# Mixture of experts behind a ring of weights: the overflow test moves into the up product

## The chip, the cores and the metric

One NeuronCore of a Trainium2 chip runs the whole program. The metric is the device time of one execution in microseconds. Before the change three runs took 1918.42, 1920.21 and 1922.09 us; the median is 1920.21.

## The reference, cut to what matters

The program is three transformer layers over 256 tokens of width 1024 in float32: a windowed attention layer and a short convolution layer, each with a feed-forward part, and a third layer with two kinds of attention and a mixture of 32 experts. The change touches the experts alone. Each token goes to 4 of 32 experts; tokens of one expert are gathered, multiplied with its up weights (1024 x 2048), put through a gated activation, multiplied with its down weights (1024 x 1024), weighted and added back:

```python
logits = (xf @ w_router + b_router)
top_v, top_i = lax.top_k(logits, TOP_K)          # 4 of 32
w = jax.nn.softmax(top_v, axis=-1)
...
h = lax.ragged_dot(xs, w_up, sizes) + b_up[sorted_e]
g, lin = jnp.split(h, 2, axis=-1)
g = jnp.minimum(g, SWIGLU_LIMIT)
lin = jnp.clip(lin, -SWIGLU_LIMIT, SWIGLU_LIMIT)
act = g * jax.nn.sigmoid(SWIGLU_ALPHA * g) * (lin + 1.0)
y = lax.ragged_dot(act, w_down, sizes) + b_down[sorted_e]
y = y * w.reshape(-1)[order][:, None].astype(y.dtype)
return jax.ops.segment_sum(y, tok, num_segments=n).reshape(B, T, D)
```

## The kernel before

All large weights pass through one ring of slots in SBUF (class Ring, lines 24 to 76). A unit is 128 partitions x 4096 floats, 2048 KB. An expert has six units: four of up weights (moe_u[e, 0] to moe_u[e, 3]; except in expert 0, unit c holds k steps 2c and 2c+1 of all columns) and two of down weights (moe_u[e, 4] and [e, 5]). While the experts run, the ring has ten slots. The units have a fixed order. Line 53 issues their transfers from SyncE; a unit is issued when the program has given a slot back (ring.done) and the last reader of the slot's old tile is done. What SyncE has to wait for is a semaphore that the reader raises; a reader inside a conditional block counts as done when the block has been left.

The loop over the experts (lines 1947 to 1978) is written out 32 times. For expert e it computes, on up to 64 tokens:

- the up product (up, line 1724): bias, then 8 k steps into the PSUM banks pg (gate) and pl (linear), each step with two column halves in two halves of the rows; 64 products of 512 columns;
- combine(pem): adds the output of expert e-1 to the accumulators (eight products);
- extra(e, 0), lines 1814 to 1856: a conditional block on the token count in a register. If the expert has more than 64 tokens, rounds of 32 further tokens are computed from the same units, with all six of them. TensorE, VectorE and ScalarE each take this branch for themselves;
- ring.done for the four up units (line 1964), then act_g and act_l on VectorE and ScalarE (lines 1738 to 1745);
- slot_dup (line 1750) writes a one-hot table ohb, and gather_part gathers half of the tokens of a later pair of experts on TensorE, with the step on line 1712 behind it on VectorE;
- act_T transposes the activation (line 1778), the copy on line 1971 writes atm; slot_T (line 1761) transposes the one-hot table and copies it to pem (line 1762); slot_w (line 1769) multiplies the slots' weights and reduces them to wslm;
- the down product (down) with its bias, then weigh (lines 1799 and 1800).

The overflow code writes pem, wslm, yh and yl, the same tiles as the main path. Of the 32 experts one has an overflow round, the ninth (number 8; counted from 0).

Two limits stand in the issues of SyncE: eight transfers at most are under way, since each issue waits for one of eight semaphores in turn, and ten slots at most are held.

Of the kernel before, what the change touches and what calls it, by code (L numbers as in the profile page):

```python
# [8 lines left out]
F32R = mybir.dt.float32r  # L9
# [3 lines left out]
ALU = mybir.AluOpType  # L13
AX = mybir.AxisListType
ET = mybir.EngineType
P = 128
# [117 lines left out]
def kernel(ctx: ExitStack, tc: tile.TileContext, a: dict, out: bass.AP):  # L134
# [100 lines left out]
    ring = Ring(nc, ringp, RING)  # L235
# [145 lines left out]
    moe_u = {}  # L381
# [43 lines left out]
    def mm(o, l, r, start, stop):  # L425
        T.matmul(o, l, r, start=start, stop=stop)  # L426
# [1256 lines left out]
    def m2(name, shape, dt=F32, bufs=1):  # L1683
        return p2.tile(list(shape), dt, tag=name, bufs=bufs, name=name)
# [24 lines left out]
    def gather_part(gi, part, bank="ps"):  # L1709
        ps = X[bank].rearrange("p (a b) -> p a b", a=4)  # L1710
        gather(ps, ohs[gi], 4 * part, 4, 128)
        V.tensor_tensor(xgs[gi % 2][:, 4 * part:4 * part + 4], ps, gain2(4 * part, 4, 128), op=ALU.mult)

    def wk(e, c, k, h):

        if (e, c) == (31, 4):
            return v8(512)(ring.take(moe_u[e, c + h]))[:, k]
        if c == 4 or e == 0:
            u = ring.take(moe_u[e, c + k // 4])
            return u.rearrange("p (k f) -> p k f", k=4)[:, k % 4, h * 512:(h + 1) * 512]  # L1720
        u = ring.take(moe_u[e, k // 2])
        return u.rearrange("p (i f) -> p i f", i=2)[:, k % 2, (c // 2 * 2 + h) * 512:(c // 2 * 2 + h + 1) * 512]

    def up(e, cs, xg, free=False):

        ps = [X["pl" if c else "pg"] for c in cs]
        for p_, c in zip(ps, cs):
            for h in range(2):
                mm(p_[h * 64:(h + 1) * 64], oh3[:, e:e + 1].to_broadcast([96, 64]),
                   bup[0:96, (c + h) * 512:(c + h + 1) * 512], True, False)  # L1730
        for k in range(8):
            for p_, c in zip(ps, cs):
                for h in range(2):
                    mm(p_[h * 64:(h + 1) * 64], xg[:, k], wk(e, c, k, h), False, k == 7)
            if free and k % 4 == 3:
                ring.done(moe_u[e, cs[0] + k // 4])

    def act_g(pg, gm, th):
        V.tensor_scalar(gm, pg, 7.0, None, op0=ALU.min)  # L1739
# [3 lines left out]
    def act_l(dst, pl, gm, li):  # L1743
        V.tensor_scalar(li, pl, 7.0, -7.0, op0=ALU.min, op1=ALU.max)
        V.scalar_tensor_tensor(dst, li, 1.0, gm, op0=ALU.add, op1=ALU.mult)  # L1745

    def four(t):
        return t.rearrange("p (q j) -> p q j", j=4)

    def slot_dup(e, io, n):  # L1750

        for tt in range(2):
            V.tensor_scalar(X["ohb"][:, tt].rearrange("p (r s) -> p r s", s=n),
                            io[:, None, :n].to_broadcast([P, 128 // n, n]), posm[:, tt, e:e + 1], None,
                            op0=ALU.is_equal)

    def slot_T(pe, bank="ps"):

        ps = X[bank].bitcast(BF16)[:, 0:256].rearrange("p (a b) -> p a b", a=2)
        for tt in range(2):  # L1760
            T.transpose(ps[:, tt], X["ohb"][:, tt], identb)
        S.copy(pe, ps)  # L1762

    def slot_w(e, wsl, bank="ps"):

        pw = X[bank][:, 256:259]
        for tt in range(2):
            mm(pw, X["ohb"][:, tt], w3[:, tt, e], tt == 0, tt == 1)
        V.tensor_reduce(wsl, pw, axis=AX.X, op=ALU.add)

    def by_rows(ac):

        return ac.rearrange("p (j q) -> p q j", j=4)

    def act_T(ac, bank):
        ps = X[bank].rearrange("p (a b) -> p a b", a=4)
        for j in range(4):
            T.transpose(ps[:, j], ac[:, j * 128:(j + 1) * 128], ident)  # L1778
        return ps
# [15 lines left out]
            for g in range(2):  # L1795
                mm(py[g * 64:(g + 1) * 64], at[:, k, g * 64:(g + 1) * 64], wk(e, 4, 4 * g + k, h), g == 1 and k == 0, k == 3)

    def weigh(wsl):
        S.activation(yy[0], X["py"], AF.Identity, scale=wsl)  # L1799
        V.scalar_tensor_tensor(yy[1], X["py"], wsl, yy[0].bitcast(F32), op0=ALU.mult, op1=ALU.subtract)  # L1800

    def combine(pe):
        for h in range(2):
            for tt in range(2):
                for i in range(2):
                    mm(accm[tt][h], pe[h * 64:(h + 1) * 64, tt], yy[i][h * 64:(h + 1) * 64], False, False)

    def combine_half(pe, h):

        for tt in range(2):  # L1810
            for i in range(2):
                mm(accm[tt][h], pe[:, tt], yy[i], False, i == 1)

    def extra(e, i):

        if i == 6:
            return
        with tc.If(rv > 64 + 32 * i, label=f"extra{e}" if i == 0 else None) as more:  # L1818
            io, xo = X["io"], X["xg"]
            V.tensor_scalar(io, iota1, float(64 + 32 * i), None, op0=ALU.add)  # L1820
            onehot(X["oh"], 1, e, io)
            ps = X["ps"].rearrange("p (a b) -> p a b", a=8)
            gather(ps, X["oh"], 0, 8, 64)
            V.tensor_tensor(xo, ps[:, :, 0:32], gain2(0, 8, 32), op=ALU.mult)
            slot_dup(e, io, 32)
            pu = X["py"]
            for c in range(4):
                mm(pu[c * 32:(c + 1) * 32], oh3[:, e:e + 1].to_broadcast([96, 32]),
                   bup[0:96, c * 512:(c + 1) * 512], True, False)
            for k in range(8):  # L1830
                for c in range(4):
                    mm(pu[c * 32:(c + 1) * 32], xo[:, k], wk(e, c // 2 * 2, k, c % 2), False, k == 7)
            slot_T(pem)
            slot_w(e, wslm)
            S.copy(by_rows(X["li"]), four(pu))
            pt = act_T(X["li"], "ps")
            gm, th, at = [t[:, 0:256].rearrange("p (a b) -> p a b", a=4) for t in (X["th"], X["li"], atm)]
            act_g(pt[:, :, 0:64], gm, th)
            act_l(at, pt[:, :, 64:128], gm, th)
            py = X["py"]  # L1840
            for n in range(2):
                mm(py[64 * n:64 * n + 32], oh3d[:, e:e + 1].to_broadcast([96, 32]), bdn3[:, n * 512:(n + 1) * 512],
                   True, False)
            for kk in range(4):
                for kp_ in range(2):
                    k = 2 * kk + kp_
                    for n in range(2):
                        o = 32 * (2 * n + kp_)
                        mm(py[o:o + 32], at[:, k % 4, (k // 4) * 32:(k // 4 + 1) * 32], wk(e, 4, k, n), kk == 0 and kp_ == 1, kk == 3)
            weigh(wslm)  # L1850
            combine(pem)
            extra(e, i + 1)
        if i == 0 and e < 31:
            with more.Else():
                foresee(e + 1)

    def embed(part):
# [11 lines left out]
        for h in range(2):  # L1869
# [4 lines left out]


    X = {"ps": pstat([P, 512]), "pg": pb(), "pl": pb(), "py": pb(),
         "oh": m2("ohx", [P, 2, 64]), "xg": m2("xgx", [P, 8, 32]), "gm": m2("gm", [P, 512]), "th": m2("th", [P, 512]),
         "li": m2("li", [P, 512]), "ohb": m2("ohb", [P, 2, 128], BF16), "io": m2("io", [P, 64])}
    atm = m2("atm", [P, 512])
    pem = m2("pem", [P, 2, 128], F32R)  # L1880
    wslm = m2("wslm", [P, 1])
    yy = (m2("yh", [P, 512], F32R), m2("yl", [P, 512], F32R))
    xgs = [m2(f"xg{i}", [P, 8, 128]) for i in range(2)]
    ohs = {0: m2("oh", [P, 2, 128], bufs=2)}
    w3 = m2("w3", [P, 2, 32, 3], BF16)
# [61 lines left out]
    for e in range(32):  # L1947
        gi, o = divmod(e, 2)
        xg = xgs[gi % 2][:, :, o * 64:(o + 1) * 64]
        rv = nc.values_load(cnt[0:1, e:e + 1], engines=engs, min_val=0, max_val=256)  # L1950
        assert moe_u[e, 5] in ring.tiles
        if o == 0 and e < 30:
            ohs[gi + 1] = m2("oh", [P, 2, 128], bufs=2)
            onehot(ohs[gi + 1], 2, e + 2, iota1)
        if e == 0:
            extra(0, 0)
            for c in (0, 2):
                up(0, (c,), xg, True)
        else:
            up(e, (0, 2), xg)  # L1960
            combine(pem)
            extra(e, 0)
            for c in range(4):
                ring.done(moe_u[e, c])
        act_g(X["pg"], X["gm"], X["th"])
        act_l(by_rows(X["li"]), four(X["pl"]), four(X["gm"]), four(atm))
        slot_dup(e, iota1, 64)
        if e < 30:
            gather_part(gi + 1, o)
        pt = act_T(X["li"], "pl")  # L1970
        S.copy(atm.rearrange("p (a b) -> p a b", a=4), pt)
        slot_T(pem, "pg")
        slot_w(e, wslm, "pg")
        if e < 31:
            down(e, atm.rearrange("p (a b) -> p a b", a=4))
            weigh(wslm)
            for c in range(4, 6):
                ring.done(moe_u[e, c])
# [195 lines left out]
```

## Time and profile before

| | |
|---|---|
| median of three runs | 1920.21 us |
| profiled execution | 1920.84 us |
| its span | 1919.1 us |
| its mean granted TensorE clock | 0.975 |
| TensorE busy (PE) | 1747.5 us, 91% |
| VectorE (DVE), ScalarE (ACT), GpSimd (POOL) | 44%, 28%, 10% |
| moved by DMA | 581.70 MB, mean 303 GB/s |

The experts take the second half of the span, from about 910 us. A matmul counts as busy while it is in the pipeline, so a high share of PE does not say that PE is what the others wait for; the chain of waits and the idle times do. Rows that end in brackets tell how long the engine had been idle before, and what ended the wait. [...]

### The profile page before, as it was taken

The numbers are of one execution on the slowest core, as the hardware profiler recorded it, in microseconds if no ns is written. First come the engines' busy times: TensorE is split into PE (matmuls) and PEld (weight loads), VectorE is DVE, ScalarE is ACT, GpSimd is POOL, SyncE is SP. The second block draws the span as 40 slices with busy tenths as digits, with TensorE's granted clock in tenths as the row PEclk, the third lists the DMA queues.
The fourth block names the chain that finished last, engine by engine and source line by source line (L and its number), as shares of the span: only waits on it lengthen the run. The fifth ranks groups of instructions, "written<-read, shape, count | busy, mean of one in ns | idle before, by whom it ended". The sixth has DMA issues, their size and how long they took to land. (4 is left out here: it accounts for less than half of the span.)

```text
span 1919.1 us, 30101 instructions
## 1 busy us (share of the span) xinstructions
PE 1747.5 (91%) x12485; PEld 1162.4 (61%) x12487; DVE 836.6 (44%) x1640; ACT 542.2 (28%) x1058; POOL 196.0 (10%) x279
## 2 busy tenths in 40 slices
PE   5989999999999999998999998899988988898886
PEld 4757999989999998868433333343333433333334
DVE  3866677666588886576222211221211211112125
ACT  3455454544355454363000000000000000000004
POOL 2220000000124331402000000000000000000003
PEclk8999999999999999899999998999999999899989
DMA  9675856488776527517799998999999999999980
GB/s 332 223 220 173 299 176 219 155 229 255 229 247 199 181 80 226 151 44 297 318 392 427 424 427 352 388 426 425 426 427 427 426 426 428 424 426 426 427 322 25
DMA packets 160415, 581.70 MB, mean 303 GB/s; under 512 B 8952, under 2 KB 84928, under 8 KB 136400
## 3 DMA queue, kind: packets, MB, share of 16 engines
q1 hardware_dynamic: 157264, 576.35, 77.8%
q0 software_dynamic: 1328, 1.67, 0.5%
q8 instruction: 133, 2.18, 0.5%
q10 hardware_dynamic: 1616, 0.90, 0.2%
q14 instruction: 74, 0.61, 0.1%
HBM read 577.84 MB, written 1.05 MB: 302 GB/s over the span
## 5 line engine op out<-in xcount | busy, mean ns | idle before, releaser
L426 PE MATMUL pb<-ring,xg 128*64 128x512 f32 x2048 | 456.1, 598 | 38.7 <-DMA ring<-in_w_up_dram 36.1
L426 PEld LDWEIGHTS pb<-ring,xg 128*64 128x64 f32 x2048 | 143.1, 138 | 333.1 <-issue 260.5
L109 DVE TENSOR_TENSOR wlo<-ring,whi 128x1024 fp32r<-128x1024 f32 x212 | 273.9, 1321 | 147.2 <-ACT whi L104 114.3
L426 PE MATMUL pb<-ring,atm 128*64 128x512 f32 (+1 forms) x1056 | 237.9, 612 | 2.1 <-DVE atm L1745 2.1
L104 ACT CAST whi<-ring 128x1024 fp32r<-128x1024 f32 x215 | 214.0, 1040 | 10.2 <-PE pa L426 5.1
L426 PE MATMUL pb<-fhi,whi 128*128 128x256 f32 x704 | 199.5, 283 | 2.0 <-DVE mods L550 2.0
L426 PE MATMUL pb<-flo,whi 128*128 128x256 f32 x704 | 200.3, 285 | 0.2 <-DVE flo L513 0.2
L426 PE MATMUL pb<-fhi,wlo 128*128 128x256 f32 x704 | 199.1, 283 | 0.0
L1739 DVE TENSOR_SCALAR gm<-pb 128x512 f32<-128x512 f32 x32 | 22.1, 692 | 391.4 <-PE pb L426 391.1
L426 PEld LDWEIGHTS pb<-ring,atm 128*64 128x64 f32 (+1 forms) x1056 | 76.9, 140 | 140.5 <-issue 134.1
L1740 ACT ACTIVATE th<-gm 128x512 f32<-128x512 f32 x32 | 20.2, 632 | 452.5 <-DVE gm L1739 452.5
L1800 DVE SCALAR_TENSOR_TENSOR yl<-pb,wslm,yh 128x512 fp32r<-128x512 f32 x34 | 25.5, 750 | 261.7 <-ACT yh L1799 148.0
L426 PEld LDWEIGHTS pb<-fhi,whi 128*128 128x128 f32 x704 | 134.8, 191 | 2.7 <-DVE mods L550 2.5
L426 PEld LDWEIGHTS pb<-flo,whi 128*128 128x128 f32 x704 | 134.9, 192 | 0.6 <-DVE flo L513 0.4
L426 PEld LDWEIGHTS pb<-fhi,wlo 128*128 128x128 f32 x704 | 135.0, 192 | 0.0
L1938 POOL TENSOR_TENSOR ring<-ring,ring 128x1024 fp32r<-128x1024 f32 x4 | 12.3, 3084 | 969.6 <-ACT ring L1937 969.6
L426 PE MATMUL pa<-ahi,wlo 128*128 128x256 f32 x352 | 99.0, 281 | 0.5 <-DVE wlo L109 0.5
L426 PE MATMUL pa<-ahi,whi 128*128 128x256 f32 x352 | 99.1, 282 | 0.0
L426 PE MATMUL pa<-alo,whi 128*128 128x256 f32 x352 | 98.0, 278 | 0.0
L1799 ACT ACTIVATE yh<-pb,wslm 128x512 fp32r<-128x512 f32 x34 | 23.4, 687 | 258.7 <-PE pb L426 258.7
L426 PE MATMUL pstat<-oh,htok 128*128 128x128 f32 x496 | 74.0, 310 | 22.0 <-PEq L1818 11.3
L426 PEld LDWEIGHTS pstat<-oh,htok 128*128 128x128 f32 x496 | 68.8, 218 | 34.9 <-issue 34.6
(587 smaller groups left out, 2868.3 us busy)
## 6 DMA issues: line engine op xcount, KB each, us to landing
ring<-in_w_up_dram SPq DMA_DIRECT2D x124, 2048.0 KB, 37.8
ring<-in_w_down_dram SPq DMA_DIRECT2D x62, 2048.0 KB, 28.7
ring<-in_ada_w_dram SPq DMA_DIRECT2D x24, 2048.0 KB, 9.1
ring<-in_ffn_w_up_dram SPq DMA_DIRECT2D x44, 1024.0 KB, 9.2
ring<-in_ffn_w_down_dram SPq DMA_DIRECT2D x10, 2048.0 KB, 8.1
ring<-in_sc_w_in_dram SPq DMA_DIRECT2D x24, 512.0 KB, 6.9
ring<-in_w_in_dram SPq DMA_DIRECT2D x4, 2048.0 KB, 10.5
ring<-in_w_up_dram SPq DMA_DIRECT2D x8, 1024.0 KB, 8.2
```

The source lines that it names most:

```text
L104: nc.scalar.copy(hs, src)
L109: (eng or nc.vector).tensor_tensor(ls, src, hs.bitcast(F32), op=ALU.subtract)
L426: T.matmul(o, l, r, start=start, stop=stop)
L1739: V.tensor_scalar(gm, pg, 7.0, None, op0=ALU.min)
L1740: S.activation(th, gm, AF.Tanh, scale=0.851)
L1799: S.activation(yy[0], X["py"], AF.Identity, scale=wsl)
L1800: V.scalar_tensor_tensor(yy[1], X["py"], wsl, yy[0].bitcast(F32), op0=ALU.mult, op1=ALU.subtract)
L1938: eng.tensor_tensor(lo[:, sl], w[:, sl], hi[:, sl].bitcast(F32), op=ALU.subtract)
```

## The change

Four edits, all in the expert loop.

- The up product is split into up_bias and four quarters of two k steps each. Behind the first quarter stands the overflow test, extra(e, 0), with slot_dup right behind it; then the other quarters. Each unit is given back behind its own quarter, the first behind the test. combine(pem) follows the fourth quarter. Expert 0 keeps its order by column halves.
- The overflow code gets tiles of its own: pex, wslx, yx. Since it now runs ahead of combine(pem), pem, yh and yl of expert e-1 are still needed then.
- slot_w moves ahead of the gather, its reduction on VectorE behind the gather's step.
- The tile gm goes; the gate's activation uses atm, and act_l's scratch is th.

```diff
-    def up(e, cs, xg, free=False):
-        ps = [X["pl" if c else "pg"] for c in cs]
-        for p_, c in zip(ps, cs):
+    def up_bias(e, cs=(0, 2)):
+        for c in cs:
...
+    def up(e, xg, ks, cs=(0, 2)):
+        for k in ks:
+            for c in cs:
                 for h in range(2):
-                    mm(p_[h * 64:(h + 1) * 64], xg[:, k], wk(e, c, k, h), False, k == 7)
-            if free and k % 4 == 3:
-                ring.done(moe_u[e, cs[0] + k // 4])
+                    mm(X["pl" if c else "pg"][h * 64:(h + 1) * 64], xg[:, k], wk(e, c, k, h), False, k == 7)
...
-        V.tensor_reduce(wsl, pw, axis=AX.X, op=ALU.add)
+        return lambda: V.tensor_reduce(wsl, pw, axis=AX.X, op=ALU.add)
...
-            slot_T(pem)
-            slot_w(e, wslm)
+            slot_T(pex)
+            slot_w(e, wslx)()
...
-            weigh(wslm)
-            combine(pem)
+            weigh(wslx, yx)
+            combine(pex, yx)
...
         else:
-            up(e, (0, 2), xg)
+            up_bias(e)
+            for c in range(4):
+                up(e, xg, (2 * c, 2 * c + 1))
+                if c == 0:
+                    extra(e, 0)
+                    slot_dup(e, iota1, 64)
+                ring.done(moe_u[e, c])
             combine(pem)
-            extra(e, 0)
-            for c in range(4):
-                ring.done(moe_u[e, c])
         act_g(X["pg"], X["gm"], X["th"])
-        act_l(by_rows(X["li"]), four(X["pl"]), four(X["gm"]), four(atm))
-        slot_dup(e, iota1, 64)
+        act_l(by_rows(X["li"]), four(X["pl"]), four(X["gm"]), four(X["th"]))
+        ws = slot_w(e, wslm, "pg")
         if e < 30:
             gather_part(gi + 1, o)
+        ws()
         pt = act_T(X["li"], "pl")
         S.copy(atm.rearrange("p (a b) -> p a b", a=4), pt)
         slot_T(pem, "pg")
-        slot_w(e, wslm, "pg")
```

What stands on TensorE in expert 1, before, from the up product to the test. The four names ring_... are the expert's up units; pa are the accumulators; ohx belongs to the overflow code.

```order
L426 MATMUL pb<-ring_10757,xg_10983 64x512 x8
L426 MATMUL pb<-ring_10905,xg_10983 64x512 x8
L426 MATMUL pb<-ring_10907,xg_10983 64x512 x8
L426 MATMUL pb<-ring_10909,xg_10983 64x512 x8
L426 MATMUL pa<-yh,pem 128x512
L426 MATMUL pa<-yl,pem 128x512
...
L1818 COMPARE_AND_BRANCH
L426 MATMUL pstat<-ohx,htok 128x64 x16
```

And of the changed kernel, the same place.

```order
L426 MATMUL pb<-ring_10757,xg_10986 64x512 x8
L1819 COMPARE_AND_BRANCH
L426 MATMUL pstat<-ohx,htok 128x64 x16
...
L1819 UNCONDITIONAL_BRANCH x6
L2182 BRANCH_PREFETCH_HINT
L1819 UNCONDITIONAL_BRANCH
L426 MATMUL pb<-ring_10905,xg_10986 64x512 x8
L426 MATMUL pb<-ring_10907,xg_10986 64x512 x8
L426 MATMUL pb<-ring_10909,xg_10986 64x512 x8
```

The test has moved ahead of the readers of three units, so that their reads lie behind the conditional block.

TensorE behind the test, before, in the same expert: from the gather to the down product. w is the table of slots' weights, bdn the down bias.

```order
L426 MATMUL pstat<-oh,htok 128x128 x8
L1778 MATMUL pb<-ident,li 128x128 x4
L1761 LDWEIGHTS ohb
L1761 MATMUL pb<-identb,ohb 128x128
...
L426 LDWEIGHTS ohb
L426 MATMUL pb<-w_10986,ohb 128x3
...
L426 LDWEIGHTS oh3d
L426 MATMUL pb<-bdn_10993,oh3d 64x512
...
L426 MATMUL pb<-ring_11693,atm 64x512 x8
L426 MATMUL pb<-ring_11703,atm 64x512 x8
```

And of the changed kernel.

```order
L426 LDWEIGHTS ohb
L426 MATMUL pb<-w_10989,ohb 128x3
...
L426 MATMUL pstat<-oh,htok 128x128 x8
L1777 MATMUL pb<-ident,li 128x128 x4
L1760 LDWEIGHTS ohb
L1760 MATMUL pb<-identb,ohb 128x128
...
L426 LDWEIGHTS oh3d
L426 MATMUL pb<-bdn_10996,oh3d 64x512
...
L426 MATMUL pb<-ring_11698,atm 64x512 x8
L426 MATMUL pb<-ring_11708,atm 64x512 x8
```

The products with w have moved from behind the transposes to ahead of the gather.

## Rows read from the trace of the kernel before

**Rows 1.** The page, part 2: the span in 40 slices.

```profile
DMA  9675856488776527517799998999999999999980
GB/s 332 223 220 173 299 176 219 155 229 255 229 247 199 181 80 226 151 44 297 318 392 427 424 427 352 388 426 425 426 427 427 426 426 428 424 426 426 427 322 25
```

**Rows 2.** Chain that ended last: start us, us, what.

```profile
1810.08 39.24 DMA ring<-in_w_up_dram
1849.37 2.82 PE pb L426 x12
```

**Rows 3.** TensorE's waits, 900 to 1860: us in total, times, longest.

```profile
PE pb L426 <- DMA ring<-in_w_up_dram: 36.1, 25, 2.2
...
PE pstat L426 <- PEq L1818: 11.3, 4, 3.4
PE pstat L426 <- DVE gm L1741: 7.7, 24, 0.4
```

**Rows 4.** Timeline, VectorE: experts 1, 7, 16 and 28 (start us, us).

```profile
959.69 0.69 DVE L1739 TENSOR_SCALAR gm<-pb 128x512 f32<-128x512 f32 x1 [11.84 <-PE pb L426]
...
1119.10 0.69 DVE L1739 TENSOR_SCALAR gm<-pb 128x512 f32<-128x512 f32 x1 [11.84 <-PE pb L426]
...
1401.24 0.69 DVE L1744 TENSOR_SCALAR atm<-pb 128x512 f32<-128x512 f32 x1
...
1764.26 0.69 DVE L1744 TENSOR_SCALAR atm<-pb 128x512 f32<-128x512 f32 x1
```

**Rows 5.** Windows: PE, PEld, DVE, ACT, POOL busy; PEclk, DMA share, GB/s.

```profile
956.00:966.00 10.00, 8.79 (x58) 4.92 (x56) 4.24 (x8) 1.49 (x3) 0.00 (x0) 1.00 0.36 117
1169.00:1181.00 12.00, 7.95 (x48) 4.27 (x41) 4.18 (x7) 1.32 (x2) 0.00 (x0) 0.78 0.38 132
1208.00:1215.00 7.00, 3.56 (x20) 3.26 (x17) 2.57 (x5) 0.00 (x0) 0.00 (x0) 0.76 0.49 157
1178.00:1184.00 6.00, 4.84 (x24) 4.65 (x24) 2.40 (x5) 0.86 (x2) 0.00 (x0) 0.50 0.93 339
1213.00:1836.00 623.00, 555.92 (x2844) 225.14 (x2845) 114.72 (x233) 46.63 (x86) 0.00 (x0) 0.98 1.01 425
```

**Rows 6.** Timeline, SyncE's issues: the first behind each hole.

```profile
924.96 3.76 SPq L53 DMA_DIRECT2D ring<-in_w_down_dram  x2
...
961.78 0.80 SPq L53 DMA_DIRECT2D ring<-in_w_down_dram  x2
...
1177.65 0.80 SPq L53 DMA_DIRECT2D ring<-in_w_down_dram  x2
...
1211.59 1.85 SPq L53 DMA_DIRECT2D ring<-in_w_down_dram  x2
```

**Rows 7.** Timeline, TensorE: experts 1, 9 and 10.

```profile
946.60 13.90 PE L426 MATMUL pb<-ring,xg 128*64 128x512 f32 x64
...
1211.77 3.46 PE L426 MATMUL pstat<-oh,htok 128*128 128x128 f32 x16 [3.44 <-PEq L1818]
...
1239.67 2.12 PE L426 MATMUL pstat<-oh,htok 128*128 128x128 f32 x16 [0.33 <-DVE gm L1741]
...
1243.22 0.19 PE L426 MATMUL pb<-w,ohb 128*128 128x3 bf16 x2 [0.88 <-ACT pem L1762]
```

**Rows 8.** Timeline, TensorE: expert 8, its last up unit and overflow body.

```profile
1146.18 3.65 PE L426 MATMUL pb<-ring,xg 128*64 128x512 f32 x16 [1.24 <-DMA ring<-in_w_up_dram]
...
1150.89 1.98 PE L426 MATMUL pstat<-ohx,htok 128*128 128x64 f32 x15
...
1167.65 4.97 PE L426 MATMUL pb<-ring,atm 128*32 128x512 f32 x32 [2.08 <-DVE atm L1745]
```

**Rows 9.** Timeline, VectorE: expert 10, behind the activation.

```profile
1241.13 0.46 DVE L1753 TENSOR_SCALAR ohb<-iota,posm 128x128 bf16<-128x128 f32 x2
1241.83 0.69 DVE L1712 TENSOR_TENSOR xg<-pstat,lnp 128x512 f32<-128x512 f32 x1 [0.23 <-PE pstat L426]
...
1243.51 0.16 DVE L1769 TENSOR_REDUCE wslm<-pb 128x1 f32<-128x3 f32 x1 [0.99 <-PE pb L426]
```

More of the change, by code (lines that the diff above doesn't have):

```diff
@@ L1722, in wk @@
         return u.rearrange("p (i f) -> p i f", i=2)[:, k % 2, (c // 2 * 2 + h) * 512:(c // 2 * 2 + h + 1) * 512]
-    def up(e, cs, xg, free=False):
-        ps = [X["pl" if c else "pg"] for c in cs]
-        for p_, c in zip(ps, cs):
+    def up_bias(e, cs=(0, 2)):
+        for c in cs:
             for h in range(2):
-                mm(p_[h * 64:(h + 1) * 64], oh3[:, e:e + 1].to_broadcast([96, 64]),
+                mm(X["pl" if c else "pg"][h * 64:(h + 1) * 64], oh3[:, e:e + 1].to_broadcast([96, 64]),
                    bup[0:96, (c + h) * 512:(c + h + 1) * 512], True, False)
-        for k in range(8):
-            for p_, c in zip(ps, cs):
+    def up(e, xg, ks, cs=(0, 2)):
+        for k in ks:
+            for c in cs:
                 for h in range(2):
-                    mm(p_[h * 64:(h + 1) * 64], xg[:, k], wk(e, c, k, h), False, k == 7)
-            if free and k % 4 == 3:
-                ring.done(moe_u[e, cs[0] + k // 4])
+                    mm(X["pl" if c else "pg"][h * 64:(h + 1) * 64], xg[:, k], wk(e, c, k, h), False, k == 7)
     def act_g(pg, gm, th):
@@ L1796, in down_half, with weigh, combine @@
                 mm(py[g * 64:(g + 1) * 64], at[:, k, g * 64:(g + 1) * 64], wk(e, 4, 4 * g + k, h), g == 1 and k == 0, k == 3)
-    def weigh(wsl):
+    def weigh(wsl, yy=None):
+        yy = yy or ym
         S.activation(yy[0], X["py"], AF.Identity, scale=wsl)
         V.scalar_tensor_tensor(yy[1], X["py"], wsl, yy[0].bitcast(F32), op0=ALU.mult, op1=ALU.subtract)
-    def combine(pe):
+    def combine(pe, yy=None):
+        yy = yy or ym
         for h in range(2):
@@ L1811, in combine_half @@
             for i in range(2):
-                mm(accm[tt][h], pe[:, tt], yy[i], False, i == 1)
+                mm(accm[tt][h], pe[:, tt], ym[i], False, i == 1)
     def extra(e, i):
@@ L1876 @@
     X = {"ps": pstat([P, 512]), "pg": pb(), "pl": pb(), "py": pb(),
-         "oh": m2("ohx", [P, 2, 64]), "xg": m2("xgx", [P, 8, 32]), "gm": m2("gm", [P, 512]), "th": m2("th", [P, 512]),
+         "oh": m2("ohx", [P, 2, 64]), "xg": m2("xgx", [P, 8, 32]), "th": m2("th", [P, 512]),
          "li": m2("li", [P, 512]), "ohb": m2("ohb", [P, 2, 128], BF16), "io": m2("io", [P, 64])}
-    atm = m2("atm", [P, 512])
+    atm = X["gm"] = m2("atm", [P, 512])
     pem = m2("pem", [P, 2, 128], F32R)
     wslm = m2("wslm", [P, 1])
-    yy = (m2("yh", [P, 512], F32R), m2("yl", [P, 512], F32R))
+    wslx = m2("wslx", [P, 1])
+    pex = m2("pex", [P, 2, 128], F32R)
+    yx = (m2("yxh", [P, 512], F32R), m2("yxl", [P, 512], F32R))
+    ym = (m2("yh", [P, 512], F32R), m2("yl", [P, 512], F32R))
     xgs = [m2(f"xg{i}", [P, 8, 128]) for i in range(2)]
@@ L1956 @@
             extra(0, 0)
+            slot_dup(0, iota1, 64)
             for c in (0, 2):
-                up(0, (c,), xg, True)
-        else:
-            up(e, (0, 2), xg)
+                up_bias(0, (c,))
+                for r in range(2):
+                    up(0, xg, range(4 * r, 4 * r + 4), (c,))
+                    ring.done(moe_u[0, c + r])
+        else:
+            up_bias(e)
[5 more added lines that the diff above has]
+                ring.done(moe_u[e, c])
             combine(pem)
-            extra(e, 0)
-            for c in range(4):
-                ring.done(moe_u[e, c])
         act_g(X["pg"], X["gm"], X["th"])
-        act_l(by_rows(X["li"]), four(X["pl"]), four(X["gm"]), four(atm))
-        slot_dup(e, iota1, 64)
+        act_l(by_rows(X["li"]), four(X["pl"]), four(X["gm"]), four(X["th"]))
+        ws = slot_w(e, wslm, "pg")
         if e < 30:
             gather_part(gi + 1, o)
+        ws()
         pt = act_T(X["li"], "pl")
```

## The prediction

> **What bounds the kernel now.** I read the page's slices first. From about the twentieth slice to the end of the experts the DMA row stands at 9 and the rate at 426 GB/s [rows 1]: the weight stream fills the second half of the kernel. The chain of waits then says that this stream also sets the end: its longest piece is the DMA of 39.24 us that was issued at 1810.08 and brought the last up unit of expert 31, and TensorE's work follows it without a break [rows 2]. The waits say the same from TensorE's side: 25 waits for up weights, 36.1 us in all [rows 3].
>
> Two paces can be read from the timeline of VectorE. While TensorE waits for nothing, the first step behind the up product comes at 959.69 in expert 1 and at 1119.10 in expert 7 [rows 4]: six experts in 159.41 us, 26.57 us each. Where the stream rules, the step on line 1744 comes at 1401.24 in expert 16 and at 1764.26 in expert 28 [rows 4]: twelve experts in 363.02 us, 30.25 us each, 5.04 us a unit. So TensorE has 3.7 us to spare per expert, and only what keeps the stream from moving costs time.
>
> Then the windows: where does the stream not move? Against 425 GB/s in the long stretch, 956 to 966 moved 117, 1169 to 1181 moved 132, and 1208 to 1215 moved 157 [rows 5]. That is 10 x (1 - 117/425) = 7.2 us, 12 x (1 - 132/425) = 8.3 us and 7 x (1 - 157/425) = 4.4 us without movement, 19.9 us in all. The issues of SyncE show why: each hole ends with a burst of issues, at 961.78, 1177.65 and 1211.59 [rows 6]. At each of these times the branch of lines 1811 to 1854 has just been passed and all four up units of an expert become free together. An earlier hole, before 924.96, belongs to expert 0, whose units the kernel gives back in the same places before and after; I leave it as it is.
>
> **What the holes cost.** What counts is when a unit has wholly landed, so I measure on landings. Number the units six to an expert. With ten slots, the four bursts issue unit 10 (924.96), unit 16 (961.78), unit 58 (1177.65) and unit 64 (1211.59). At 5.04 us a unit the steps should have been 6, 42 and 6 units, that is 30.25, 211.8 and 30.25 us; they were 36.82, 215.87 and 33.94. The holes cost 6.6, 4.1 and 3.7 us, 14.4 us together. The pace holds to the end: from 1211.59 to the last up unit, number 189, are 126 units or 635 us, which gives 1846.9 for its landing before the latency of the first transfer, and the row says 1849.37 [rows 2].
>
> **The change, part by part.**
>
> *Units given back one by one.* Expert 1's up product begins at 946.60 and takes 13.9 us [rows 7], 3.5 us a quarter. With the branch behind it the first unit is free at about 951, the others 3.5 us apart. The stream runs dry at 956, and each release buys it 5.04 us. The first hole closes wholly: -6.6 us. SyncE's queue has nothing else between these issues.
>
> *The test behind the first quarter.* One expert overflows, the ninth (number 8). Its overflow body runs from 1150.89 to the release at 1177.65, 26.8 us [rows 6, 8]. Now it starts behind the first quarter. The step on line 1739 comes 13.1 us into an up product (946.60 to 959.69), so the next product begins 26.57 - 13.1 = 13.5 us behind that step: for expert 8 at 1119.10 + 13.5 = 1132.6. The quarter ends at 1136.1 and the body at 1162.9. The body needs all six units of the expert; the up units arrived by 1146.18 before [rows 8] and come 6.6 us sooner now, and the body reaches its down product 16.8 us after its start (1150.89 to 1167.65), at 1152.9, when the down units, 10 us behind, are there. The unbroken stream wants slot 58 at 924.96 + 48 x 5.04 = 1167. The release at 1162.9 is 4 us early. [...] I charge 1.0 us, with 0 and 6 as the ends (all of it on time; or the body's exit and the slow clock 5 us longer): -7.8 + 1.0 = -6.8 us.
>
> *The branch inside the up product.* It now stops TensorE between two quarters in every expert. At its old place the gap was 0.33 us, and 3.44 at the worst [rows 7]. [...]
>
> *Slots' weights ahead of the gather, own tiles.* The two small products move ahead of the gather (+0.19 us, their length). Behind the transposes TensorE waited 0.88 us for the copy of pem [rows 7]; the down product then needs only the copy of atm. The transposes of the slots now stand behind the reduction on VectorE, which follows xg (1241.83 + 0.69 + 0.16 = 1242.7 [rows 9]), so about 0.35 us of the 0.88 are kept. Together a TensorE expert is unchanged within 0.4 us. Without slack this would be up to 12 us; the 36.1 us of waits hide it. Only in the last expert, which has no gather and lies behind the last landing, does it show: -0.4 us. VectorE's slot_dup (0.46 us) leaves the chain between li and xg, which TensorE's gather covers; merging gm into atm adds no wait, since atm's readers are done an expert earlier.
>
> **The sum.** -6.6 - 6.8 - 0.4 = -13.8 us. The profiled execution took 1920.84 us (span 1919.1 and 1.7 around it), 0.6 above the median of 1920.21; 1920.84 - 13.8 = 1907.0, and I predict 1907 us.
>
> [...] In 24 experts the wait behind the jump over the overflow code was 0.4 us at most, 7.7 us in all; in four it was 11.3 us in all, 3.4 at most [rows 3]. [...]
>
> **The rivals.**
>
> *Slower: the jump stalls every expert.* Place: between the first and second quarter. [...] Price: 3.44 us in 31 experts, 107 us; the 36.1 us of waits for weights absorb the first part. It decides from 36.1/31 = 1.2 us an expert: below it the kernel is not slower. At the full price 1920.8 + 107 - 36 = 1991 us. For it: the four long waits. Against: the 24 short ones. Chance 0.05.
>
> *No change: a net 1.2 us an expert.* The same mechanism at half strength, or expert rows lengthened by the new wait on the reduction, eats exactly the slack: 1920. Above 0.7 us an expert ((36.1 - 14.4)/31) the forecast begins to shrink. Chance 0.07.
>
> *Only the first hole closes.* The overflow body now holds four quarters' worth of units instead of following them, and if its exit comes 5 us later than I reckon, new holes of 4 to 8 us open behind 1163: 1920.8 - 6.6 - 0.4 = 1914 us. [...] Against: the body's own length is from the row. Chance 0.15.
>
> *All 19.9 us come back.* The 5.04 us a unit are the slowest of the DMA engines; by the mean rate a unit of 2048 KB takes 4.93 us. If the lag comes from the holes and not from the engines, the gain is 19.9 + 0.4: 1900.5 us. For it: within one expert the units land 4.89 us apart (3.65 + 1.24 [rows 8]). Against: 30.25 us an expert over twelve experts without a hole. Chance 0.13.
>
> **How the numbers follow.** Forecast 0.60 (its own range 1903 to 1911), the rivals 0.05, 0.07, 0.15 and 0.13. What a measurement of this kernel can tell from no change is about 0.2%, 3.8 us. Faster takes the forecast, the first-hole case and the full 19.9: 0.88; same 0.07; slower 0.05. The range reaches from the full return with 1.5 us to spare, 1899, to the first-hole case, 1914; the two cases outside it hold 0.12.
>
> **What would show it.** Right: no burst of issues at one time, but up units issued about 3.5 or 4.9 us apart from expert 1 on; the DMA rate at 420 or more from 930 to about 1825 with at most a shallow dip near 1165 to 1200; the last up unit of expert 31 landing near 1836; TensorE waiting for weights before the last quarter in more than half of the experts. Wrong: a gap above 1 us between the first and second quarter in most experts; a hole behind the overflow as wide as the old one; or a last landing at 1836 with an end that did not move with it, which would make the 71 us behind the landing a bound of their own.

## The result, and the profile after

The changed kernel took 1908.17 us, median of four runs (1905.98 to 1909.23); the kernel before, run beside it, took 1919.35 us. The ratio is 0.994, with the 95% interval [0.9928, 0.9953]. Forecast were 1907 us and a range of 1899 to 1914.

The slices of the page, after. Compare the nineteenth to the twenty-sixth with [rows 1]:

```profile
DMA  9575955488776518615899999999999999999970
GB/s 328 207 231 158 332 177 193 145 242 244 255 239 217 176 45 250 177 45 225 370 426 425 426 425 426 426 425 425 427 426 426 427 426 425 426 426 426 421 263 26
```

The two dips of 352 and 388 GB/s that stood in the middle of the experts are gone. The windows of the three holes [rows 5], after (PE, PEld, DVE, ACT, POOL busy; PEclk, which is TensorE's granted clock as a share of its full speed, DMA share, GB/s):

```profile
956.00:966.00 10.00, 9.81 (x62) 5.25 (x60) 3.90 (x6) 1.50 (x3) 0.00 (x0) 1.00 1.00 424
1169.00:1181.00 12.00, 11.81 (x70) 5.56 (x68) 3.32 (x6) 1.55 (x3) 0.00 (x0) 1.00 1.01 431
1208.00:1215.00 7.00, 6.84 (x36) 2.36 (x34) 2.12 (x7) 0.69 (x1) 0.00 (x0) 1.00 1.02 428
```

117, 132 and 157 GB/s have become 424, 431 and 428. SyncE's issues show how; these answer to the bursts at 961.78 and 1177.65 [rows 6]:

```profile
949.47 4.04 SPq L53 DMA_DIRECT2D ring<-in_w_down_dram  x2
956.61 15.46 SPq L53 DMA_DIRECT2D ring<-in_w_up_dram  x4
...
1157.32 4.42 SPq L53 DMA_DIRECT2D ring<-in_w_down_dram  x2
```

Into expert 1's six slots units are now issued over 22 us, as each slot comes free. In the overflowing expert the first slot comes free at 1157.32, 20 us earlier. The chain that ended last begins as it did [rows 2], with the last up unit landing 11.3 us earlier:

```profile
1797.99 40.05 DMA ring<-in_w_up_dram
1838.09 2.82 PE pb L426 x12
```

TensorE, expert 1 (first two rows) and the overflowing expert 8 (last two), at the branch that now stands in the up product:

```profile
945.73 3.60 PE L426 MATMUL pb<-ring,xg 128*64 128x512 f32 x16
949.49 10.52 PE L426 MATMUL pb<-ring,xg 128*64 128x512 f32 x48 [0.17 <-PEq L1819]
...
1132.91 3.98 PE L426 MATMUL pstat<-ohx,htok 128*128 128x64 f32 x32
...
1157.72 10.52 PE L426 MATMUL pb<-ring,xg 128*64 128x512 f32 x48 [0.52 <-PEq L1819]
```

The gap in the brackets is the price of the branch in its new place, in the last row that of leaving the overflow body. TensorE's waits, 900 to 1860 (us in all, times, longest), which answer to [rows 3]:

```profile
PE pb L426 <- DMA ring<-in_w_up_dram: 51.3, 37, 2.2
PE pb L1760 <- DVE wslm L1768: 5.8, 30, 0.4
PE pb L426 <- PEq L1819: 5.8, 21, 2.2
```

The gaps that these rows lay to the branch come to 5.8 us, where they were 11.3 at the old place. TensorE waits for weights in 37 places instead of 25: the stream rules for longer.

### The profile page after: what moved, and what is told of

It reads as the page before. It is cut to its first block, busy times and chain, and to the rows that moved or that the text cites. A ratio compares the mean times of both kernels' runs of the same rounds, so it can differ in the third digit from the quotient of the medians.

```text
span 1905.9 us, 30232 instructions
## 1 busy us (share of the span) xinstructions
PE 1757.6 (92%) x12487; PEld 1162.9 (61%) x12487; DVE 840.9 (44%) x1640; ACT 542.7 (28%) x1058; POOL 196.0 (10%) x279
## 5 line engine op out<-in xcount | busy, mean ns | idle before, releaser
L426 PE MATMUL pb<-ring,xg 128*64 128x512 f32 x2048 | 470.7, 608 | 58.3 <-DMA ring<-in_w_up_dram 51.3
L426 PEld LDWEIGHTS pb<-ring,xg 128*64 128x64 f32 x2048 | 154.7, 139 | 355.1 <-issue 255.4
L426 PE MATMUL pb<-ring,atm 128*64 128x512 f32 (+1 forms) x1056 | 233.4, 604 | 2.3 <-DVE atm L1744 2.1
L1738 DVE TENSOR_SCALAR atm<-pb 128x512 f32<-128x512 f32 x32 | 22.1, 691 | 353.5 <-PE pb L426 353.5
L1739 ACT ACTIVATE th<-atm 128x512 f32<-128x512 f32 x32 | 20.2, 632 | 498.6 <-DVE atm L1738 498.6
L426 PEld LDWEIGHTS pb<-ring,atm 128*64 128x64 f32 (+1 forms) x1056 | 72.9, 137 | 139.1 <-issue 129.6
L426 PE MATMUL pstat<-oh,htok 128*128 128x128 f32 x496 | 67.5, 291 | 0.0
L426 PEld LDWEIGHTS pa<-ahi,wlo 128*128 128x128 f32 x352 | 66.1, 188 | 1.0 <-DVE wlo L109 1.0
```

The costliest lines, as they stand in the source:

```text
L1739: S.activation(th, gm, AF.Tanh, scale=0.851)
```

## The experiments

**Which part of the change gives the gain.** First the giving back alone. All four units are given back behind the fourth quarter, while the test stays behind the first:

```diff
+            for c in range(4):
                 ring.done(moe_u[e, c])
```

> The changed kernel with all four up units given back together behind the fourth quarter; the overflow test stays behind the first. Theory: a transfer waits for the last reader of the slot's old unit, whatever the place of the give-back in the program, so nothing changes: 1908 us, SyncE's issues in expert 1 still spread from about 949 to 962. Rival: the place of the give-back decides; then the hole at 956 comes back (6.6 us) and part of the one behind the overflow: 1915 to 1918 us.

Measured: 1908.33 us, ratio to the kernel before 0.9935 [0.9922, 0.9949], and the same issue times (949.46 for expert 1). So with the test behind the first quarter the last reader of a slot sets the time of the next issue, and the place of the give-back in the program made no difference. The lines that give units back could have stayed together behind the up product.

Then the test alone, moved behind the fourth quarter again (c == 3) or behind the third (c == 2), with each quarter's unit given back no earlier than the test:

```diff
-                if c == 0:
+                if c == 3:
```

> The changed kernel with the overflow test behind the fourth quarter and the units given back behind it, all else as changed (slots' weights ahead of the gather, own tiles). Theory: the place of the test is the whole gain in the stream, so the three holes come back (14 us by the old trace, 11 by the moved landing) and only the shorter end behind the last landing (0.6 us) stays: 1918 to 1919 us. Rival: the gain comes from TensorE's shorter expert (26.24 for 26.57 us) and the moved slots' weights: 1908 us.

Measured: 1916.1 us, 0.998 [0.9971, 0.9989]. Two of the three holes are back (windows of this kernel):

```profile
956.00:966.00 10.00, 8.66 (x54) 4.69 (x52) 4.08 (x8) 1.49 (x3) 0.00 (x0) 1.00 0.61 223
1146.00:1171.00 25.00, 20.77 (x156) 8.68 (x152) 2.67 (x8) 2.37 (x4) 0.00 (x0) 0.93 0.89 378
1169.00:1181.00 12.00, 8.24 (x50) 5.34 (x43) 4.68 (x8) 1.32 (x2) 0.00 (x0) 0.85 0.43 152
1208.00:1215.00 7.00, 6.83 (x35) 3.85 (x36) 2.24 (x4) 0.86 (x2) 0.00 (x0) 0.84 1.01 431
```

So some 8 of the 11 us hang on the place of the test. The first hole is narrower than before (223 instead of 117 GB/s) and the third is gone, which the expectation had not allowed for. In this run the test also stands ahead of combine(pem), whose eight products take 1.2 us and stood ahead of it before; expert 1's first slot is issued again at 959.12 instead of 961.78. Whether this makes the other 3 us is not shown.

> The changed kernel with the overflow test behind the third quarter, three units given back behind it. Theory: what counts is whether a release comes before the stream runs dry. In expert 1 the first three units come free at about 957, the stream is dry at 956 and needs 1.7 us to start: a hole of 2 to 3 us; behind the overflow the release at about 1164 is still ahead of the 1167 that the stream wants. So 2.5 us are lost against the changed kernel: 1910.5 us. Rival: each quarter that the test moves back costs its share of the gain: two of three quarters, 7 us, 1915 us.

Measured: 1906.49 us, 0.9928 [0.9915, 0.9942], no hole from 956 to 966 (429 GB/s). The expectation missed: the third quarter is early enough. The start of a stopped stream, which it put at 1.7 us, was about right (before, 15 packets are under way 1.6 us behind the issue at 961.78), but little of it was lost: counted from the first issue behind expert 0, unit 16 landed 1.1 us later than in the changed kernel, the last up unit 0.3 us. That the run looks faster than the changed kernel is not its doing. In its profile the experts begin 4.2 us earlier (first issue behind expert 0 at 920.30 instead of 924.52), and from the activation of expert 0 to that of expert 31 it takes 913.27 us, the changed kernel 912.97.

**What the overflow body costs.** In the kernel before, and then in the changed one, the test is set above 255, so that no expert enters the body:

```diff
-        with tc.If(rv > 64 + 32 * i, ...
+        with tc.If(rv > 255 - i * 0, ...
```

> The kernel before with the overflow test set above 255 tokens, so the body is never entered; left out are the tokens beyond 64 of the one expert that overflows. The code and its branches stay. Theory: the two holes behind the overflow (4.1 and 3.7 us) go, the hole in expert 1 stays: 1911.5 us. Rival one: the overflow costs its 26.8 us of TensorE time: 1892 us. Rival two: the stream sets the end and hides the overflow: 1919 us, no change.

Measured: 1910.92 us, 0.9948 [0.9934, 0.9961]. As expected the first hole stays (114 GB/s) and the other two, which are the body's, are gone (426 and 424 GB/s).

> The changed kernel with the test set above 255, so that the overflow body is never entered (the tokens beyond 64 of the one overflowing expert are left out). Theory: with the change the body no longer runs the ring dry (the stretches 1169 to 1181 and 1208 to 1215 move 431 and 428 GB/s in the changed kernel), so that taking the body away gives nothing: 1908, between 1906.5 and 1909.5, and the last up unit lands at the same 1838. Rival: the weights that wait for their places during the 24.4 us of the body still cost landings that the mean rate hides, and the 2 to 3 us by which the last landing came later than forecast are theirs: 1904.5 to 1906, the last up unit landing near 1835.

Measured: 1907.03 us, 0.9925 [0.9911, 0.994]; the last up unit lands at 1837.82. Theory right: 24 us of work taken out give 1.1 us, inside the intervals. Without the body SyncE issues unit 58 21.7 us earlier, but unit 95 only 0.9 us earlier, as much as it was ahead at unit 10, before the body. What the engines save in this expert the stream takes back. From unit 10 on the changed kernel is bound by the stream.

**The slots' weights, put back behind the transposes.**

```diff
-        ws = slot_w(e, wslm, "pg")
...
-        ws()
...
         slot_T(pem, "pg")
+        slot_w(e, wslm, "pg")()
```

> The changed kernel with the slots' weights put back behind the transposes of the slots, as before the change; all else as changed. Theory: the stream of the weights rules, so that the order of these small steps matters only behind the last landing, where it gave some 0.5 us (from the landing to the first product of the last half 8.6 us before and 8.0 after): 1908.7, between 1907 and 1910. Rival: the steps lie on the way from one expert to the next in the twelve experts in which TensorE still leads, at 0.3 us each: 1911 to 1912.

Measured: 1907.39 us, 0.9929 [0.9914, 0.9945]: no difference that can be told. TensorE then waits 26.7 us in all for the copy of pem instead of 5.8 us for the reduction, beside the stream.

**Why a unit takes 5.06 us when the DMA engines move 2 MB in 4.9.** The forecast took the pace from a row and left its cause alone. SyncE's issues from 1525 to 1561, after; each starts 0.06 us behind the landing eight transfers back:

```profile
1524.98 0.33 SPq L53 DMA_DIRECT2D ring<-in_w_up_dram  x1
1530.86 0.33 SPq L53 DMA_DIRECT2D ring<-in_w_down_dram  x1
1535.74 0.33 SPq L53 DMA_DIRECT2D ring<-in_w_down_dram  x1
1540.63 0.33 SPq L53 DMA_DIRECT2D ring<-in_w_up_dram  x1
1545.54 0.33 SPq L53 DMA_DIRECT2D ring<-in_w_up_dram  x1
1550.42 0.33 SPq L53 DMA_DIRECT2D ring<-in_w_up_dram  x1
1555.32 0.33 SPq L53 DMA_DIRECT2D ring<-in_w_up_dram  x1
1561.19 0.33 SPq L53 DMA_DIRECT2D ring<-in_w_down_dram  x1
```

Between two steps of 5.88 and 5.87 us lie five of 4.88 to 4.91, and so in each expert. Between 1400 and 1800 the queues of the DMA engines carried, beside the weights (packets, MB, share of 16 engines):

```profile
q8 instruction: 27, 0.44, 0.5%
q14 instruction: 22, 0.18, 0.1%
```

The profile names the kind of both queues instruction. In the five experts from 1464 to 1592 each long step begins within 2 us of one or two q14 packets. The overflow code is long (six nested rounds in each of 32 experts), and all of it but one round is jumped over. So I cut it to one round:

```diff
-        if i == 6:
+        if i == 1:
             return
```

> The changed kernel with the overflow code cut from six nested rounds to one (for more than 96 tokens on an expert the rest would be left out; with these inputs no expert has so many). Each expert's landings show five steps of 4.9 us and one of 5.9. Theory: the sixth is held back by the instruction packets that the same DMA engines carry, some 3.7 an expert; with 43 in 100 of TensorE's instructions gone from the program fewer are fetched, the step shrinks, and up to 0.4 us an expert come back over the some 20 experts in which the stream rules: 1900 to 1906. Rival: an expert that doesn't enter its body fetches what it runs and no more, however long the body is, or the late step has another cause: 1906.5 to 1909.5, and as many instruction packets as before.

Measured: 1888.16 us, 0.9832 [0.9817, 0.9848], 20 us less than the changed kernel and beyond what the theory had asked for. The long step is gone from nearly every expert (from unit 16 to the last up unit 7 steps of the landings are over 5.3 us, in the changed kernel 29); this kernel's issues from 1521 to 1550, and its instruction packets from 1400 to 1800:

```profile
1521.12 0.33 SPq L53 DMA_DIRECT2D ring<-in_w_down_dram  x1
1526.01 0.33 SPq L53 DMA_DIRECT2D ring<-in_w_up_dram  x1
1530.90 0.33 SPq L53 DMA_DIRECT2D ring<-in_w_up_dram  x1
...
1545.58 0.33 SPq L53 DMA_DIRECT2D ring<-in_w_down_dram  x1
1550.48 0.33 SPq L53 DMA_DIRECT2D ring<-in_w_down_dram  x1
```

```profile
q8 instruction: 27, 0.44, 0.5%
q14 instruction: 8, 0.07, 0.0%
```

Then no overflow code at all, in which the hints ahead of the branch and VectorE's and ScalarE's loading of the counts go too (TensorE still loads them):

```diff
     def extra(e, i):
-        if i == 6:
-            return
+        return
```

> The changed kernel with the overflow code, its test and the loading of the counts into the engines' registers taken out altogether (the tokens beyond 64 of the one overflowing expert are left out). Theory of the instruction packets: with no code to jump over the packets of an expert fall, and with them the long step of its landings (5.9 us beside five of 4.9): 1893 to 1904, against the kernel that has the code and never enters it. Rival: the long step stays, since the code that every expert runs is fetched all the same: 1906.5 to 1909.5. The gap of TensorE at the branch (0.17 to 2.2 us in the changed kernel) is gone in either case, and gives nothing where the stream rules.

Measured: 1879.9 us, 0.9788 [0.9774, 0.9802]. Against the kernel that has the code and never enters it (1907.03) that is 27.1 us, more than the theory asked for. The long steps account for nearly all of it: from unit 16 to the last up unit that kernel has 29 steps over 5.3 us, which are 29.0 us longer than as many of 4.89, this one 3, which are 3.9 us longer, and the stretch is 24.0 us shorter (875.6 and 851.6). The runs do not separate the code's share of the last 8 us from that of the hints and the loading. Its instruction packets from 1400 to 1800:

```profile
q8 instruction: 14, 0.23, 0.2%
q14 instruction: 5, 0.04, 0.0%
```

The mean rate of the stream hides all this: 426 GB/s in the changed kernel, 427 with one round. It shows at the end of the stream, in the last windows before the last landing. These rows are the changed kernel:

```profile
1824.00:1832.00 8.00, 7.83 (x38) 2.52 (x34) 1.23 (x3) 0.69 (x1) 0.00 (x0) 1.00 0.13 51
1826.00:1832.00 6.00, 5.83 (x28) 1.70 (x23) 0.48 (x2) 0.00 (x0) 0.00 (x0) 1.00 0.06 25
```

and this the kernel with one round:

```profile
1804.00:1812.00 8.00, 7.84 (x40) 2.71 (x38) 1.23 (x3) 0.69 (x1) 0.00 (x0) 1.00 1.00 410
```

With the long code 0.06 of 16 engines, that is one, is still at work 6 to 12 us ahead of the last landing; the others are done. With the short code all sixteen work nearly to the end. The landings tell the same. In the trace each transfer raises its semaphore sixteen times, read here as once by each engine: for the last up unit of the changed kernel the first fifteen came 16.9 to 30.7 us ahead of the sixteenth (5.0 to 9.8 us at unit 64), and with one round the fifteenth came 0.1 us ahead of it. A unit has landed when its slowest part has, so one engine that falls behind the first of the sixteen by about a microsecond an expert (9.8 us at unit 64, 30.7 some 21 experts later) sets the time, while the mean hardly moves.

**What makes the packets.** Without the hints that name the next branch:

```diff
     def foresee(e):
-        tc.mark_branch_hint_location(f"extra{e}", "LikelyTaken", engs)
+        return
```

> The changed kernel without the hints that name the next expert's branch as likely taken. Theory one: it is the hint that makes the engines fetch the jump's target ahead, in packets of their own on the DMA engines; without it these packets and the late landing of each expert go: 1890 to 1900 in the stretch in which the stream rules, less what the gaps at the branch take in the first twelve experts. Theory two: the target is fetched in either case, without the hint only at the jump; the late landing stays, and TensorE's gap at the branch grows from 0.2 to some 2 us in the experts in which TensorE leads: 1909 to 1930.

Measured: 1965.26 us, 1.0229 [1.0213, 1.0244], worse than theory two allowed. TensorE's waits of this kernel:

```profile
PE pb L426 <- PEq L1819: 82.3, 32, 4.2
```

2.6 us at the branch in each expert, instead of 5.8 us in all. The packets stay: 74 on q14 in the whole run, where the changed kernel has 78, and 163 on q8 instead of 131. So the hint does not cause the packets. With it TensorE's branch itself is shorter; the changed kernel's branches from 1400 to 1800 (PEldq is TensorE's sequencer; ns, shortest, median, longest) and, second, this kernel's:

```profile
L1819 PEldq COMPARE_BRANCH  x13: 349/359/2312, 1429.6 to 1793.9; - x13
L1819 PEldq COMPARE_BRANCH  x14: 6033/6282/6458, 1400.2 to 1793.1; - x14
```

Of a branch of 6.3 us the gap shows 2.6; the other 3.7 us lie, by my estimate, under the first quarter's products, which take 3.60 us. VectorE's branches take 0.06 us in the changed kernel. What TensorE does in the 6.3 us is not shown.

**Versions that take any number of tokens.** Three rounds of 64 tokens instead of six of 32, first with the test ahead of the up product:

```diff
-        if i == 6:
+        if i == 3:
...
-        with tc.If(rv > 64 + 32 * i, ...
+        with tc.If(rv > 64 + 64 * i, ...
...
+            extra(e, 0)
             up_bias(e)
```

> A version meant to be used: the changed kernel with the overflow in three nested rounds of 64 tokens, where six of 32 were, built from the functions of the ordinary expert, and with its test ahead of the up product (the two banks of the up product are free there). It still takes any number of tokens up to 256; TensorE's program stands between the one of six rounds and the one of one round (10497 rows beside 14127 and 8077). Theory (the late landing, once an expert, comes from the instruction packets, and these from the length of the code that is jumped): on the line between the changed kernel at 1908.2 and the one of one round at 1888.2 it comes to 1896, and with both ends 1889 to 1902. Rival: any jump beyond one packet costs the same late landing, and the branch at the head of the expert adds its gap: 1906 to 1911. The body's place costs nothing in either, since the first up unit is given back after body and first quarter, as in the changed kernel.

Measured: 1958.84 us, 1.0198 [1.0183, 1.0214], outside what either expected. TensorE's waits show a new one:

```profile
PE pb L426 <- DVEq L1819: 73.4, 30, 7.6
```

2.4 us in each of 30 experts. At the head of the expert VectorE comes to its own branch only behind the last weighing of the expert before (its step on line 1800 starts at 1528.41, TensorE's next product at 1529.48), and TensorE, which takes the same branch, waits for it. Behind the first quarter, I reckoned, the wait would lie under the quarter's 3.6 us. So the same rounds with the test there, in the banks ps and py:

```diff
+            X["pg"], X["pl"] = X["ps"], X["py"]
             up_bias(e)
             up(e, xo, range(8))
...
                 if c == 0:
                     extra(e, 0)
```

> A version meant to be used: the changed kernel, its test behind the first quarter of the up product as it is, but the overflow in three nested rounds of 64 tokens, where six of 32 were; the rounds use the gather's and the down product's banks, since the up product's hold its first quarter. It takes any number of tokens up to 256. TensorE's program has 11613 rows (the changed kernel 14127, the one with one round 8077). Theory (the late landing of each expert depends on the length of code that is jumped): on the line between 1908.2 and 1888.2 it comes to 1900, with the ends 1889 and 1904. Rival: only code short enough to be fetched along with what stands ahead of it is free, and three rounds are too long for it: 1906.5 to 1909.5, with a long step of landings per expert as before. The head of the expert, where the test cost 2.4 us at each expert in the version with the test ahead of the up product (TensorE waits there for VectorE's branch behind the last weighing), is free of it: no gap over 0.6 us at the branch in most experts.

Measured: 1899.72 us, 0.9898 [0.9877, 0.9918], as the theory had it, and TensorE's waits for VectorE's branch in each expert are gone. But the body now takes 39 us, and the stream waits for it (this kernel's window):

```profile
1160.00:1186.00 26.00, 24.27 (x122) 9.82 (x120) 5.13 (x9) 2.13 (x4) 0.00 (x0) 0.96 0.64 258
```

Hence one round of 32, and three nested ones of 64 behind it:

```diff
+    def wider(e, i):
+        if i == 4:
+            return
+        with tc.If(rv > 32 + 64 * i):
...
-            extra(e, i + 1)
+            wider(e, 1)
```

> The changed kernel with one overflow round of 32 tokens, as it is, and behind it three nested rounds of 64 for what is left, so that any number up to 256 is taken with four rounds instead of six. The version with three rounds of 64 came to 1899.7; there the body that these inputs enter took 39 us instead of 24, no weight was asked for between 1128 and 1170, and the stretch from 1160 to 1186 moved 258 GB/s. Here the body is again the short one, so that this hole goes, worth some 9 us of transfers; TensorE's program has 12824 rows (the changed kernel 14127, three rounds of 64 11613, one of 32 8077). Theory one (the number of late landings falls steeply once the code is some shorter, and the hole cost three rounds of 64 some 5 us): 1891 to 1898. Theory two (cost proportional to the length jumped): 1904, between 1901 and 1906, slower than three rounds of 64 in spite of the hole.

Measured: 1895.95 us, 0.9872 [0.9856, 0.9889]: theory one, and the lowest time of the versions that take any number of tokens, 12 us below the changed kernel; the interval overlaps that of the three rounds of 64. Its q14 packets from 1400 to 1800 are 14, where there were 22, and from 1450 to 1800 it has 8 long steps instead of 11. These inputs enter the first round alone, so the rounds of 64 behind it were not timed.

## Why the prediction was right

- *What bounds the kernel.* Right. The stream sets the end, and only holes in it cost time. The overflow body shows it best: in the kernel before taking it out gave 8 to 10 us, in the changed one 1.1 us between two medians.
- *The first hole closes.* Right, in size too: counted from the issue of unit 10 (924.96 before, 924.52 after), unit 16 landed 6.4 us sooner (at 969.67 before, 962.88 after), where 6.6 were forecast. How much of it reaches the end is less sure: the two kernels without overflow, with and without this hole, lie 3.9 us apart, with intervals of some 2.7 us to either side.
- *The test behind the first quarter.* Right, and with more room than reckoned. The body ran from 1132.91 and gave the first slot back at 1157.32, not at 1162.9: TensorE's experts before it had become a little shorter (959.19 to 1116.61 for six, 26.24 us each instead of 26.57), and from the body's first product to the release it took 24.4 us instead of 26.8. The body's products took as long as before (24.3 us, before 24.5); TensorE's branch at their end took 0.37 us instead of 3.27, on which the forecast had not counted. The granted clock of 0.50 behind the body [rows 5] did not come either: from 1157.7 to 1168.3 it was 1.00, and the 48 products there took 10.52 us, as in expert 1. In expert 9, behind a gap of 2.23 us at the branch (3.44 before [rows 7]), 48 products took 12.22 us at a granted clock of 0.86. None of this held the stream up: counted as above, unit 64 landed 13.2 us sooner (1219.24 and 1205.63), forecast were 13.4 for the two parts. The 1.0 us that the sum charges behind the body is shown by no run: unit 58 landed at 1175.31 and unit 64 at 1205.63, six units in 30.3 us, the pace of the stretch without holes.
- *Why it works.* Where the reasoning spoke of releases one by one, the run with late releases (1908.33 us, expert 1's first issue at 949.46 beside 949.47) shows that the last reader decides here. The move of the test did both.
- *The branch.* The sum has no term for it. In its new place the gap is 0.17 us in the common row and 2.2 at the worst, 5.8 us in all over 21 places. A price in every expert shows only in the run without hints: there each pays 2.6 us, behind a branch of 6.3. With the hint the median branch of TensorE takes 0.36 us. So the slower rivals fell.
- *The end behind the last landing.* 0.4 us were taken. From the last landing to the end it became 1.8 us shorter, 71.5 to 69.7. Some 0.6 are the moved products. The rest goes with TensorE's clock, which the sum had left out: from the bias product to the last product of the last half it took 6.41 us before and 5.24 after; granted were 0.67 over 1858 to 1866 before, and 0.77 over the answering stretch, 1846 to 1852, after.
- *The pace.* This is the term that was mis-sized, by about 2 us: the last up unit landed 11.3 us earlier and not 13.4. Expert 15 to expert 30 take 30.35 us each, where 30.25 had been read [rows 4], and 126 units at that pace make 2.1 us more. The landings agree: from unit 64 to the last up unit the kernel before took 630.1 us and the changed one 632.4, with 21 steps over 5.3 us instead of 19. Behind the holes of the kernel before the slowest engine was level with the others: at unit 64 the last of the sixteen came 0.1 us behind the fifteenth, in the changed kernel 5.0. That this makes the two steps is not shown. The rows of VectorE:

```profile
1356.60 0.69 DVE L1738 TENSOR_SCALAR atm<-pb 128x512 f32<-128x512 f32 x1 [10.97 <-PE pb L426]
...
1811.82 0.69 DVE L1738 TENSOR_SCALAR atm<-pb 128x512 f32<-128x512 f32 x1 [13.33 <-PE pb L426]
```

- *The number.* That 1907 came so near is in part luck: the stream gave 2.1 us less than reckoned, and the end behind it 1.4 us more. From one profiled execution to the other it became 13.1 us less, where 13.8 were forecast; between the medians, 11.2.
- *The rival in which all 19.9 us come back* fell: it laid the lag of the slowest engines to the holes. The lag stays when the holes are closed, and has grown: for the last up unit the last of the sixteen came 9.7 us behind the fifteenth before and 16.9 after. It goes with the length of the code that is jumped over: with one round the last came 0.1 us behind. That code, never entered, cost 27.1 us with its test and hints (1907.03 and 1879.9), where all holes were put at 14.4.

What stays open is how a packet of 8 KB, which at an engine's share of the rate (426/16 = 27 GB/s) would take 0.3 us and in the trace takes 0.3 to 0.45, costs its engine about 1 us, and whether it is the packet that does it: with one round three long steps are left behind 1400 (6.34 to 6.37 us), of which one has no q14 packet within 2 us, and most of the eight q14 packets have no long step beside them. In that kernel eight engines lead the last by 3 us and more at 1684, and a delay to one of these would cost no landing; that this is the reason was not tested. Shown is that here less code to jump over went with fewer packets and a shorter time: 22 packets on q14 from 1400 to 1800 in the changed kernel at 1908.17 us, 14 with four rounds at 1895.95, 8 with one at 1888.16, 5 with none at 1879.9; and with fewer late landings, 29 in the changed kernel, 7 with one round, 3 with none.

## What to carry to other kernels

In a ring of weights, look for the last reader of each slot, and for what stands ahead of it. Here the rare branch belonged inside the product, ahead of its last piece, where slots still came free in time and other engines' branches were covered: behind the first quarter the kernel took 1908.17 us, behind the third 1906.49, behind the fourth 1916.1, and at the head of the expert, with three rounds of 64, 1958.84 where the same rounds behind the first quarter took 1899.72. With the weight stream as the bound, code that was jumped over was not free (20 us from six rounds to one), and the time between issues showed it (5.88 us beside 4.89), not the mean rate (426 and 427 GB/s). So try a rare path in few wide rounds, with the likeliest one kept short: one round of 32 and three of 64 took 1895.95 us.

## What the runs showed of the hardware that I had not expected

- Overflow code that is never entered cost, with its test, its hints and most of the loading of the counts, 27 us of 1907 here. In the changed kernel one of the sixteen DMA engines, as the landings are read here, falls behind, by 16.9 us at the last up unit; the mean rate differs by 1 to 2 GB/s.
- A hint ahead of a branch was worth 57 us (1965.26 against 1908.17). Without it TensorE's median branch took 6.3 us instead of 0.36, and its gaps grew by 76 us, part of which waits for weights had covered.
- The branch that three engines take coupled them: with the test at the head of the expert TensorE waited 2.4 us in each of 30 experts for VectorE's branch; with it behind the first quarter, 3.6 us of TensorE's work, that wait was gone from each expert.
